# Large experts: gates and their turn between the two ways up, last combination by token halves, splits of the next stage issued in the last two experts

## Chip, cores and metric

One core of one Trainium2 chip. The metric is the device time of one execution in microseconds; the median of three runs of the kernel before is 2007.82 us.

## The reference, cut to what matters

The program is a chain of three blocks: a layer with attention and a dense feed-forward network, a layer with attention and eight large experts, and a hybrid block with 32 small experts. Only the large experts and the layer norm behind them are touched. Each of 256 tokens goes to its best two of eight experts of width 2816:

```python
def moe_swiglu(x, w_router, b_router, w_in, w_out):
    logits = (x2 @ w_router).astype(jnp.float32) + b_router.astype(jnp.float32)
    top_vals, top_idx = lax.top_k(logits, TOP_K)
    gates = jax.nn.softmax(top_vals, axis=-1)
    ...
    def expert_block(args):
        xb, e = args
        h = xb @ w_in[e]
        return (jax.nn.silu(h[:, :D_FF]) * h[:, D_FF:]) @ w_out[e]
    ...
    y = jnp.zeros_like(x2).at[slot_tok].add((ys * slot_gate[:, None]).astype(x2.dtype))

x = layer_norm(DN_ALPHA * x + ffn, ln_ffn_g[i], ln_ffn_b[i])
```

## The kernel before

The order of every engine's instructions is the order in which the program emits them; nothing is reordered later. Each engine, and each DMA queue, takes its own in that order. Nearly all DMAs are issued by SyncE (SP).

**Weights.** Two streams share SP. `Long` (L159) brings the weights of the large experts as tiles of 128 x 2816 floats, `wl`, 1408 KB each, through eight buffers; `get` hands out the next tile and `load` issues the next load as soon as the tile before the one in use is given up, so SP then waits for TensorE. `Stream` (L32) brings all other weights as tiles of 512 KB, `wr`, through four raw buffers at this point. Most of them are split into two parts, `ws`, the high one by a copy on ScalarE (L123) and the low one by a subtraction on VectorE (L124), through three split buffers here. `ahead` (L133) alternates loads and splits until a buffer is lacking; a raw buffer is used again once its tile has been split. A row of a layer norm keeps its raw buffer until the norm is finished. With `eager` set, each `get` calls `ahead` first.

**The stage `moe1`** (L1223). The end of the norm before, routing (logits, ranks, slots: one-hot `OH` of 256 tokens by 96 slots for each expert, gates `G`), and a gather: x is split into `xth` (ScalarE) and `xtl` (GpSimd, POOL), and 64 matmuls pick the tokens of all experts into `gx`. Then the loop over eight experts (L1372), with a ring of eight PSUM banks. An expert uses 24 tiles `wl`: eight for the first way up (`pa`, then Silu on ScalarE), eight for the second (`pb`, then the gating product on VectorE, L1383, and a block transpose on VectorE into `ehT`, L1384, for three groups `g` of 32 slots), and eight for the way down. Every matmul there is a 32-column one; four run beside each other on four column groups (`c`). Between the ways up and the way down stand `combine` of the expert before (its outputs `ey` by its turned gates `mOT`, added to x by VectorE, L1369) and `back` (L1330): VectorE multiplies the one-hot by the gate into `mog` (L1336), TensorE turns it in six transposes, and ScalarE copies it to `mOT`. The way down goes through 22 steps `j`, each over the three groups and four chunks (L1393 to L1402).

**The end of the stage** (L1407). Combine of the last expert, four adds of 512 columns over both token halves; `get` of the norm's rows, which calls `ahead`, since `eager` was set in the last expert: first blocks of the hybrid stage are loaded and split here, ahead of the norm's statistics in the queue of VectorE. The statistics come one by one (L517, L522), the norm of token half 0 at once (L530), that of half 1 in the next stage (`finish`). The hybrid stage (L2289) turns x (L321: transposes, `xh` on ScalarE, `xl` on VectorE) and multiplies.

Of the kernel before, what the change touches and what calls it, by code (L numbers as in the profile page):

```python
# [10 lines left out]
F32 = mybir.dt.float32  # L11
# [8 lines left out]
T = 256  # L20
D = 1024
# [1201 lines left out]
def moe1(k, A, x, alpha, before, br):  # L1223
# [3 lines left out]
    with ExitStack() as mo:  # L1227
# [8 lines left out]
        with ExitStack() as ro:  # L1236
            ro.enter_context(k.banks(g=2, t=2, acc=4))
            rp = ro.enter_context(k.pool(name="m1r", bufs=1))
            xth = rp.tile([128, 2, D], F32R, name="xth")
            xtl = rp.tile([128, 2, D], F32R, name="xtl")  # L1240
            xT = rp.tile([128, KD, T], F32, name="mxT")
            lg = rp.tile([128, 2, NE], F32, name="mlg")
            lgT = rp.tile([NE, T], F32, name="mlgT")

            def gather(q):

                for j in range(KD):
                    p = k.g() if j % 2 else k.t()
                    n = 4 * CAP
                    for i, src in enumerate((xth, xtl)):  # L1250
                        for tb in range(2):
                            w = src[:, tb].rearrange("p (c j) -> p j c", j=KD)[:, j]
                            k.pe.matmul(p[:, :n], w, OH[:, tb, 4 * q:4 * q + 4].rearrange("p e s -> p (e s)"),
                                        start=i == 0 and tb == 0, stop=i == 1 and tb == 1)
                    k.copy(gx[:, j, 4 * q:4 * q + 4], p[:, :n].rearrange("p (e s) -> p e s", e=4))

            (wr, _, _), = k.st.get("rt")
            k.long.load()
            for tb in range(2):
                turn_half(k, x, xT, tb)  # L1260
                if tb == 0:
                    before.finish()
                    ln = LayerNorm(k, x, 1.0, "nm")
                p = k.g()
                ts = slice(tb * 128, tb * 128 + 128)
                for j in range(8):
                    k.pe.matmul(p[:NE, :128], wr[:, j], xT[:, j, ts], start=j == 0, stop=j == 7)
                nc.vector.tensor_copy(lgT[:, ts], p[:NE, :128])
                k.pe.transpose(p[:, 256:256 + NE], lgT[:, ts], k.ident[:NE, :NE])
                nc.vector.tensor_add(lg[:, tb], p[:, 256:256 + NE], br)  # L1270
                nc.scalar.copy(xth[:, tb], x[:, tb])
                nc.gpsimd.tensor_sub(xtl[:, tb], x[:, tb], xth[:, tb].bitcast(F32))
            rank = ranks(k, rp, lg, NE, "m1")
            M = rp.tile([128, 2, NE], BF, name="mM")
            nc.vector.tensor_scalar(M, rank, 1.5, None, op0=OP.is_lt)
            pos, count = places(k, rp, M, NE)

            slot = rp.tile([128, 2, NE], F32, name="mslot")
            nc.vector.tensor_scalar(slot, M, -65536.0, 65536.0, op0=OP.mult, op1=OP.add)
            nc.vector.tensor_add(slot, slot, pos)  # L1280

            def places_of(a, b):
                n = b - a
                nc.vector.tensor_tensor(
                    OH[:, :, a:b], k.iota[:, :CAP].rearrange("p (u o s) -> p u o s", u=1, o=1).to_broadcast([128, 2, n, CAP]),
                    slot[:, :, a:b].rearrange("p b (e o) -> p b e o", o=1).to_broadcast([128, 2, n, CAP]), op=OP.is_equal)

            places_of(0, 4)
            nc.vector.tensor_scalar(over, pos, float(CAP) - 0.5, None, op0=OP.is_gt)
            cf = rp.tile([128, 1], F32, name="mcf")  # L1290
            nc.vector.tensor_reduce(out=cf, in_=count, op=OP.max, axis=AX.X)
            nc.vector.tensor_copy(cnt, cf)
            gather(0)
            places_of(4, NE)

            oh = rp.tile([128, 2, 2, NE], F32, name="moh")
            mx = rp.tile([128, 2, 8], F32, name="mmx")
            gs = rp.tile([128, 4, 2], F32, name="mgs")
            for i in range(2):
                nc.gpsimd.tensor_scalar(oh[:, i], rank, float(i), None, op0=OP.is_equal)  # L1300
            for tb in range(2):
                nc.vector.max(out=mx[:, tb], in_=lg[:, tb])
            nc.gpsimd.tensor_sub(gs[:, 0], mx[:, :, 1], mx[:, :, 0])
            nc.scalar.activation(gs[:, 1], gs[:, 0], AF.Exp)
            nc.gpsimd.tensor_scalar(gs[:, 0], gs[:, 1], 1.0, None, op0=OP.add)
            nc.vector.reciprocal(gs[:, 2], gs[:, 0])
            nc.gpsimd.tensor_mul(gs[:, 3], gs[:, 1], gs[:, 2])
            w2 = [gs[:, 2 + i].rearrange("p (b o) -> p b o", o=1).to_broadcast([128, 2, NE]) for i in range(2)]
            nc.gpsimd.tensor_mul(G, oh[:, 0], w2[0])
            nc.gpsimd.tensor_mul(oh[:, 1], oh[:, 1], w2[1])  # L1310
            nc.gpsimd.tensor_add(G, G, oh[:, 1])
            nc.gpsimd.tensor_mul(over, over, G)
            gather(1)
            for tb in range(2):
                nc.scalar.mul(x[:, tb], x[:, tb], alpha)
            nv = nc.values_load(cnt[0:1, 0:1], min_val=0, max_val=T)
            with tc.If(nv > CAP):  # L1317
                wi, wo = (A[n].rearrange("l e a b -> (l e) a b") for n in ("w_exp_in", "w_exp_out"))
                leftover(k, x, xT, over, NE, KF,
                         lambda e, j: [wi[ds(e, 1), :, i * DFF + j * 128:i * DFF + j * 128 + 128].rearrange(  # L1320
                             "o (k p) n -> (o p) k n", p=128) for i in range(2)],
                         lambda e, j: wo[ds(e, 1), j * 128:j * 128 + 128].rearrange("o p n -> (o p) n"))
# [4 lines left out]
        tl = lambda shape, name, bufs=1: ep.tile(shape, F32, name=name, tag=name, bufs=bufs)  # L1327
        H2 = HF // 2

        def back(e):  # L1330

            t = tl([128, NG, T], "mOT", 2)
            og = tl([128, 2, NG, 4, 32], "mog")
            for tb in range(2):
                src = OH[:, tb, e].bitcast(F32).rearrange("p (g o s) -> p g o s", g=NG, o=1)
                nc.vector.tensor_scalar(og[:, tb], src.to_broadcast([128, NG, 4, 32]), G[:, tb, e:e + 1], None, op0=OP.mult)  # L1336
            for a in range(0, NG, 2):
                p = bank()
                n = min(2, NG - a)
# [16 lines left out]
                                        start=j == 0, stop=j == KD - 1)  # L1356
            return ps

        def combine(y, OT, after=None):
            ps = [bank() for _ in range(4)]  # L1360
            for tb in range(2):
                for g in range(NG):
                    for c in range(4):
                        cs = slice(32 * c, 32 * c + 32)
                        k.pe.matmul(ps[c][:, tb * 256:tb * 256 + 256], OT[cs, g, tb * 128:tb * 128 + 128], y[cs, g],
                                    start=g == 0, stop=g == NG - 1)
            for c in range(4):
                r = x[:, :, c * 256:c * 256 + 256]
                nc.vector.tensor_add(r, r, ps[c].rearrange("p (b n) -> p b n", b=2))  # L1369

        last = None
        for e in range(NE):  # L1372
            h = tl([128, NG, HF], "eh")
            hT = tl([128, NG, KF, 32], "ehT")
            pa = up(e)
            for g in range(NG):
                for s in range(2):
                    nc.scalar.activation(h[:, g, s * H2:s * H2 + H2], pa[g][s], AF.Silu)  # L1378
            pb = up(e)
            for g in range(NG):  # L1380
                for s in range(2):
# [2 lines left out]
                nc.vector.transpose(hT[:, g], h[:, g].rearrange("p (r j) -> p j r", j=KF))  # L1384
            if last:
                combine(*last)
            OT = back(e)
            if e == NE - 1:
                k.st.eager = True
            y = tl([128, NG, 256], "ey", 2)  # L1390
            ps = [bank()[:, :256] for _ in range(NG)]
            w = None
            for j in range(KF):  # L1393
                ws = []
                for c in range(4):
                    i = (4 * j + c) % 11
                    if i == 0:
                        w = k.long.get(c == 0)
                    ws.append(w[:, i * 256:i * 256 + 256])
                for g in range(NG):  # L1400
                    for c in range(4):
                        k.pe.matmul(ps[g][32 * c:32 * c + 32], hT[:, g, j], ws[c], start=j == 0, stop=j == KF - 1)  # L1402
                k.long.load()
            for g in range(NG):
                nc.scalar.copy(y[:, g], ps[g])  # L1405
            last = y, OT
        combine(*last)  # L1407
        ln.take([w[0] for w in k.st.get(*ln.keys)])
        for n in range(2):
            for tb in range(2):  # L1410
                ln.add(tb, n, None)
    return ln


# [1385 lines left out]
```

## Time and profile before

| | |
|---|---|
| median of 3 runs | 2007.82 us (2001.58 to 2016.43) |
| the profiled execution | 2008.52 us |
| its span, first to last instruction | 2006.7 us |
| mean granted TensorE clock | 0.946 |
| TensorE busy (matmul) | 1781.4 us, 89% |
| VectorE, ScalarE, GpSimd busy | 702.7, 448.3, 372.6 us |
| moved by DMA | 515.99 MB, mean 257 GB/s |

Times in the rows are microseconds from the start of the span. PE is TensorE's matmul, PEld its weight load, DVE VectorE, ACT ScalarE, POOL GpSimd, SPq the issuing of DMAs by SyncE. A busy PE is one with matmuls in flight; the granted clock is given as a share of 2.4 GHz. Since a matmul in float32 is two instructions, 264 matmuls are 528 instructions.

### The profile page before, as it was taken

To read this page: it belongs to the slowest core of one execution; us is meant where nothing else is said; L and a number is where in the kernel's file an instruction comes from. 1 tells how busy PE (TensorE), PEld (TensorE's weight loads), DVE (VectorE), ACT (ScalarE), POOL (GpSimd) and SP (SyncE) were. 2 spreads that over 40 slices of the span, in tenths; PEclk is the share of its full clock that TensorE was granted. 3 is DMA by queue.
4 is the path that set the end of the run, shared out by engine and by line. 5 is a ranking of instruction groups with operands and counts; after the bars stand their busy time and mean duration, and the time that the engine had idled before them with its cause. 6 is when DMAs were issued, how large, how long until landed. Compare 5 with 4: busy or idle time off the path is not lost. (4 is left out here: it accounts for less than half of the span.)

```text
span 2006.7 us, 41916 instructions
## 1 busy us (share of the span) xinstructions
PE 1781.4 (89%) x18587; PEld 1186.4 (59%) x18587; DVE 702.7 (35%) x1079; ACT 448.3 (22%) x783; POOL 372.6 (19%) x636
## 2 busy tenths in 40 slices
PE   8989999898889898989898989879765989989886
PEld 7867887896644444444444444468544767776543
DVE  5558556554110202020202020256535575621102
ACT  5534443552100000000000000033323432211100
POOL 5312987101000000000000000063213242000001
PEclk9999999899999999999999999989877999979999
DMA  6526666447489797979797979375224233799997
GB/s 217 157 65 210 203 202 204 128 119 270 171 341 403 304 412 311 411 304 412 308 413 302 414 308 415 119 237 174 86 68 149 89 98 98 276 354 408 409 408 307
DMA packets 138588, 515.99 MB, mean 257 GB/s; under 512 B 22248, under 2 KB 51350, under 8 KB 112800
## 3 DMA queue, kind: packets, MB, share of 16 engines
q1 hardware_dynamic: 135120, 497.39, 66.4%
q0 software_dynamic: 3280, 15.83, 2.3%
q8 instruction: 149, 2.44, 0.5%
q14 instruction: 39, 0.32, 0.0%
HBM read 503.48 MB, written 7.87 MB: 255 GB/s over the span
## 5 line engine op out<-in xcount | busy, mean ns | idle before, releaser
L218 PE MATMUL bank_r<-wl,gx 128*32 128x352 f32 x6144 | 455.8, 459 | 1.4 <-PEq L1317 1.4
L218 PE MATMUL bank_g<-ws,xh 128*128 128x256 f32 (+2 forms) x1440 | 387.0, 349 | 11.8 <-DVE ws L124 4.1
L218 PEld LDWEIGHTS bank_r<-wl,gx 128*32 128x32 f32 x6144 | 190.9, 110 | 263.6 <-issue 229.4
L124 DVE TENSOR_TENSOR ws<-wr,ws 128x1024 fp32r<-128x1024 f32 (+1 forms) x200 | 257.2, 1297 | 144.6 <-ACT ws L123 144.3
L218 PEld LDWEIGHTS bank_g<-ws,xh 128*128 128x128 f32 x1440 | 256.1, 194 | 50.1 <-issue 6.9
L1383 DVE TENSOR_TENSOR eh<-eh,bank_r 128x352 f32<-128x352 f32 x48 | 22.9, 505 | 654.6 <-PE bank_r L218 654.0
L123 ACT ACTIVATE ws<-wr 128x1024 fp32r<-128x1024 f32 (+1 forms) x200 | 209.2, 1057 | 175.8 <-PE bank_g L218 111.6
L218 PE MATMUL bank_r<-wl,ehT 128*32 128x256 f32 x4224 | 241.8, 393 | 0.0
L218 PE MATMUL bank_g<-ws,xl 128*128 128x256 f32 (+2 forms) x720 | 234.8, 342 | 3.4 <-DVE xl L341 3.3
L218 PEld LDWEIGHTS bank_r<-wl,ehT 128*32 128x32 f32 x4224 | 130.2, 114 | 110.4 <-issue 13.1
L533 POOL TENSOR_SCALAR lnmv<-lnmv 128x1 f32<-128x1 f32 x10 | 7.7, 772 | 887.9 <-DVE lnmv L532 887.9
L218 PEld LDWEIGHTS bank_g<-ws,xl 128*128 128x128 f32 x720 | 139.8, 194 | 17.7 <-DVE xl L341 4.4
L218 PE MATMUL bank_g<-wr,xgx 128*32 128x256 f32 x864 | 65.3, 396 | 18.9 <-DMA wr<-in_expert_w_up_dram 7.1
L1344 ACT COPY mOT<-bank_r 128x512 f32<-128x512 f32 (+1 forms) x16 | 6.9, 482 | 299.5 <-PE bank_r L222 299.5
L1378 ACT ACTIVATE eh<-bank_r 128x352 f32<-128x352 f32 x48 | 22.3, 464 | 203.9 <-PE bank_r L218 198.8
L218 PE MATMUL bank_t<-xOH,x 128*128 128x128 f32 x256 | 63.3, 409 | 0.9 <-DVE xOH L2573 0.9
L218 PEld LDWEIGHTS bank_t<-xOH,x 128*128 128x128 f32 x256 | 61.8, 336 | 3.8 <-issue 2.9
L218 PEld LDWEIGHTS bank_g<-wr,xgx 128*32 128x32 f32 x864 | 30.4, 113 | 53.2 <-DMA wr<-in_expert_w_up_dram 12.4
L1405 ACT COPY ey<-bank_r 128x256 f32<-128x256 f32 x24 | 8.9, 372 | 231.9 <-PE bank_r L218 231.3
L218 PE MATMUL bank_g<-ws,hh 128*128 128x512 f32 x176 | 57.5, 399 | 0.0
L615 POOL TENSOR_TENSOR aP<-aP,ast 128x512 f32<-128x512 f32 (+1 forms) x20 | 24.9, 1243 | 173.3 <-DVE ast L613 132.1
L222 PE MATMUL bank_r<-ident,mog 128*128 128x128 f32 x48 | 14.1, 433 | 45.7 <-DVE mog L1336 45.7
(697 smaller groups left out, 2186.1 us busy)
## 6 DMA issues: line engine op xcount, KB each, us to landing
wl<-in_w_exp_in_dram SPq DMA_DIRECT2D x128, 1408.0 KB, 9.0
wl<-in_w_exp_out_dram SPq DMA_DIRECT2D x64, 1408.0 KB, 8.5
wr<-in_expert_w_gate_dram SPq DMA_DIRECT2D x56, 512.0 KB, 10.2
wr<-in_w_in_dram SPq DMA_DIRECT2D x54, 512.0 KB, 5.0
wr<-in_expert_w_down_dram SPq DMA_DIRECT2D x54, 512.0 KB, 10.2
wr<-in_expert_w_up_dram SPq DMA_DIRECT2D x52, 512.0 KB, 10.2
wr<-in_w_ffn_in_dram SPq DMA_DIRECT2D x44, 512.0 KB, 3.9
wr<-in_w_out_dram SPq DMA_DIRECT2D x24, 512.0 KB, 4.3
```

The source lines that it names most:

```text
L123: nc.scalar.activation(hv, v, AF.Copy)
L124: nc.vector.tensor_sub(lv, v, hv.bitcast(F32))
L218: self.nc.tensor.matmul(out, lhsT, rhs, start=start, stop=stop)
L222: self.nc.tensor.transpose(out, src, ident)
L533: nc.gpsimd.tensor_scalar(mv[:, 2:3], mv[:, 1:2], 1e-5, None, op0=OP.add)
L615: e.tensor_mul(P[:, hs, :nk], P[:, hs, :nk], st[:, 3, hs].rearrange("p (h o) -> p h o", o=1).to_broadcast([128, 2, nk]))
L1344: nc.scalar.copy(t[:, a:a + n], p[:, :n * 256].rearrange("p (g t) -> p g t", g=n))
L1378: nc.scalar.activation(h[:, g, s * H2:s * H2 + H2], pa[g][s], AF.Silu)
L1383: nc.vector.tensor_mul(v, v, pb[g][s])
L1405: nc.scalar.copy(y[:, g], ps[g])
```

## The change

What it does:

1. `gates(e)`: `mog` is written by VectorE before the first way up of its expert. `back`, the six transposes and the copies to `mOT`, stands between the two ways up; before, both stood after the combine.
2. In experts 6 and 7 `ahead` is called between the two ways up. `eager` is set only when the stage is over.
3. The way down takes its first four steps `j` as one piece, group by group; from the fifth on step by step as before.
4. The last combine works by token halves: for each half the matmuls, four adds of 256 columns, the statistics, and for half 0 the norm. The norm's rows are fetched ahead of it.
5. `xth` and `xtl` are stored in the order in which the gather reads them; the stride that was in its weight reads is now in the reads of x by ScalarE and GpSimd.
6. The logits are copied from PSUM by ScalarE instead of VectorE.

```diff
-            xth = rp.tile([128, 2, D], F32R, name="xth")
-            xtl = rp.tile([128, 2, D], F32R, name="xtl")
+            xth = rp.tile([128, 2, KD, 128], F32R, name="xth")
+            xtl = rp.tile([128, 2, KD, 128], F32R, name="xtl")
...
-                            w = src[:, tb].rearrange("p (c j) -> p j c", j=KD)[:, j]
-                            k.pe.matmul(p[:, :n], w, OH[:, tb, 4 * q:4 * q + 4].rearrange("p e s -> p (e s)"),
+                            k.pe.matmul(p[:, :n], src[:, tb, j], OH[:, tb, 4 * q:4 * q + 4].rearrange("p e s -> p (e s)"),
...
-                nc.vector.tensor_copy(lgT[:, ts], p[:NE, :128])
+                nc.scalar.copy(lgT[:, ts], p[:NE, :128])
...
-                nc.scalar.copy(xth[:, tb], x[:, tb])
-                nc.gpsimd.tensor_sub(xtl[:, tb], x[:, tb], xth[:, tb].bitcast(F32))
+                xv = x[:, tb].rearrange("p (c j) -> p j c", j=KD)
+                nc.scalar.copy(xth[:, tb], xv)
+                nc.gpsimd.tensor_sub(xtl[:, tb], xv, xth[:, tb].bitcast(F32))
...
-        def back(e):
-
-            t = tl([128, NG, T], "mOT", 2)
+        def gates(e):
+
             og = tl([128, 2, NG, 4, 32], "mog")
...
+            return og
+
+        def back(og):
+
+            t = tl([128, NG, T], "mOT", 2)
...
-        def combine(y, OT, after=None):
+        def combine(y, OT, norm=None):
...
+                if norm:
+                    for c in range(4):
+                        r = x[:, tb, c * 256:c * 256 + 256]
+                        nc.vector.tensor_add(r, r, ps[c][:, tb * 256:tb * 256 + 256])
+                        if c % 2:
+                            norm.add(tb, c // 2, None)
+            if norm:
+                return
...
+            og = gates(e)
             pa = up(e)
...
+            OT = back(og)
+            if e >= NE - 2:
+                k.st.ahead()
             pb = up(e)
...
-            OT = back(e)
-            if e == NE - 1:
-                k.st.eager = True
...
-            for j in range(KF):
-                ws = []
-                for c in range(4):
-                    i = (4 * j + c) % 11
-                    if i == 0:
-                        w = k.long.get(c == 0)
-                    ws.append(w[:, i * 256:i * 256 + 256])
+
+            for js in [range(0, 4)] + [range(j, j + 1) for j in range(4, KF)]:
+                ws = {}
+                for j in js:
+                    for c in range(4):
+                        i = (4 * j + c) % 11
+                        if i == 0:
+                            w = k.long.get(len(ws) == 0)
+                        ws[j, c] = w[:, i * 256:i * 256 + 256]
                 for g in range(NG):
-                    for c in range(4):
-                        k.pe.matmul(ps[g][32 * c:32 * c + 32], hT[:, g, j], ws[c], start=j == 0, stop=j == KF - 1)
+                    for j in js:
+                        for c in range(4):
+                            k.pe.matmul(ps[g][32 * c:32 * c + 32], hT[:, g, j], ws[j, c], start=j == 0, stop=j == KF - 1)
                 k.long.load()
...
-        combine(*last)
         ln.take([w[0] for w in k.st.get(*ln.keys)])
-        for n in range(2):
-            for tb in range(2):
-                ln.add(tb, n, None)
+        combine(*last, norm=ln)
+    k.st.eager = True
     return ln
```

## Rows read from the trace of the kernel before

**Rows 1.** Timeline of TensorE: start, length, instructions, [idle time before, its end].

```profile
524.03 57.01 PE L218 MATMUL bank_r<-wl,gx 128*32 128x352 f32 x768 [1.41 <-PEq L1317]
...
674.90 2.87 PE L218 MATMUL bank_r<-ey,mOT 32*128 32x256 f32 x48
683.44 1.76 PE L222 MATMUL bank_r<-ident,mog 128*128 128x128 f32 x6 [5.67 <-DVE mog L1336]
...
1299.23 2.87 PE L218 MATMUL bank_r<-ey,mOT 32*128 32x256 f32 x48
```

**Rows 2.** Timeline of VectorE at the turn of expert 1.

```profile
673.31 1.79 DVE L1384 STREAM_TRANSPOSE ehT<-eh 128x704 f32<-128x704 f32 x1
...
675.97 1.79 DVE L1384 STREAM_TRANSPOSE ehT<-eh 128x704 f32<-128x704 f32 x1
...
678.63 1.79 DVE L1384 STREAM_TRANSPOSE ehT<-eh 128x704 f32<-128x704 f32 x1
...
682.70 1.12 DVE L1336 TENSOR_SCALAR mog<-mOH,mG 128x384 f32<-128x384 f32 x2
```

**Rows 3.** Windows: stretch, length, five engines' busy time, granted clock, DMA share, GB/s.

```profile
715.65:772.50 56.85, 56.85 (x772) 22.92 (x764) 2.58 (x3) 3.35 (x8) 0.00 (x0) 1.00 1.01 415
685.10:689.00 3.90, 3.90 (x41) 1.80 (x44) 0.00 (x0) 0.57 (x2) 0.00 (x0) 0.50 0.00 0
```

**Rows 4.** Timeline of TensorE's weight loads in the way down of expert 1.

```profile
688.97 26.36 PEld L218 LDWEIGHTS bank_r<-wl,ehT 128*32 128x32 f32 x488 [0.23 <-issue]
```

**Rows 5.** Timeline of ScalarE at the end of a first way up.

```profile
643.69 3.42 ACT L1378 ACTIVATE eh<-bank_r 128x352 f32<-128x352 f32 x6 [25.07 <-PE bank_r L218]
```

**Rows 6.** The page's DMA issues: count, KB each, median us to landing.

```profile
wl<-in_w_exp_in_dram SPq DMA_DIRECT2D x128, 1408.0 KB, 9.0
...
wr<-in_w_in_dram SPq DMA_DIRECT2D x54, 512.0 KB, 5.0
```

**Rows 7.** Timeline after the last combine, all engines.

```profile
1302.12 2.48 DVE L1369 TENSOR_TENSOR x<-x,bank_r 128x512 f32<-128x512 f32 x4 [35.02 <-PE bank_r L218]
...
1305.77 6.52 SPq L107 DMA_DIRECT2D wr<-in_w_in_dram  x3
1309.58 1.06 ACT L123 ACTIVATE ws<-wr 128x1024 fp32r<-128x1024 f32 x1 [7.93 <-DMA wr<-in_w_in_dram]
1310.67 1.23 DVE L124 TENSOR_TENSOR ws<-wr,ws 128x1024 fp32r<-128x1024 f32 x1 [3.79 <-ACT ws L123]
1311.81 1.87 DVE L522 BATCH_NORM_STATS2 lnst<-x 128x6 f32<-128x512 f32 x3
...
1313.71 0.21 DVE L532 BATCH_NORM_AGGREGATE lnmv<-lnst 128x2 f32<-128x12 f32 x1
...
1316.37 1.09 PE L222 MATMUL bank_t<-ident,x 128*128 128x128 f32 x4 [14.27 <-DVE x L539]
...
1318.19 0.67 DVE L341 TENSOR_TENSOR xl<-bank_t,xh 128x512 fp32r<-128x512 f32 x1
```

**Rows 8.** Timeline of routing and gather, all engines.

```profile
490.95 2.33 POOL L1272 TENSOR_TENSOR xtl<-x,xth 128x1024 fp32r<-128x1024 f32 x1
491.01 2.82 DVE L539 SCALAR_TENSOR_TENSOR x<-x,lnmv,wr 128x512 f32<-128x512 f32 x1 [0.75 <-POOL lnmv L534]
...
498.21 1.05 ACT L1271 CAST xth<-x 128x1024 fp32r<-128x1024 f32 x1
...
515.72 0.64 PE L218 MATMUL bank_g<-mOH,xth 128*128 128x384 f32 x2
...
521.51 0.64 PE L218 MATMUL bank_g<-mOH,xth 128*128 128x384 f32 x2
```

**Rows 9.** Groups by line, shapes kept apart: count, busy us, mean ns, idle before.

```profile
L218 PEld LDWEIGHTS bank_g<-mOH,xtl 128*128 128x128 f32 x16 | 4.7, 339 | 0.0
...
L218 PEld LDWEIGHTS bank_g<-ws,oh 128*128 128x128 f32 x32 | 6.0, 188 | 1.5 <-issue 0.2
...
L340 ACT CAST hy<-bank_t 128x512 fp32r<-128x512 f32 x2 | 2.0, 1097 | 3.5 <-PE bank_t L222 3.5
```

More of the change, by code (lines that the diff above doesn't have):

```diff
@@ L1386, in moe1 @@
                 combine(*last)
-            OT = back(e)
-            if e == NE - 1:
-                k.st.eager = True
             y = tl([128, NG, 256], "ey", 2)
             ps = [bank()[:, :256] for _ in range(NG)]
-            w = None
-            for j in range(KF):
-                ws = []
-                for c in range(4):
-                    i = (4 * j + c) % 11
-                    if i == 0:
-                        w = k.long.get(c == 0)
-                    ws.append(w[:, i * 256:i * 256 + 256])
+            for js in [range(0, 4)] + [range(j, j + 1) for j in range(4, KF)]:
[6 more added lines that the diff above has]
+                        ws[j, c] = w[:, i * 256:i * 256 + 256]
                 for g in range(NG):
-                    for c in range(4):
-                        k.pe.matmul(ps[g][32 * c:32 * c + 32], hT[:, g, j], ws[c], start=j == 0, stop=j == KF - 1)
+                    for j in js:
+                        for c in range(4):
+                            k.pe.matmul(ps[g][32 * c:32 * c + 32], hT[:, g, j], ws[j, c], start=j == 0, stop=j == KF - 1)
                 k.long.load()
```

## The prediction

> **What bounds the kernel now.** I read TensorE's timeline through the eight experts first, then VectorE's at one turn, then clock and supply by stretches, and last the two ends of the stage. The eight experts take from 524.03 to 1299.23, 775.2 us of the profiled execution, 96.9 us each [rows 1]. TensorE never waits for a weight tile there: the two ways up are one unbroken run of 57.0 us, and the way down follows at its own pace. The only hole is the turn between them: after the combine (2.87 us) TensorE stands still for 5.67 us, until the gated one-hot `mog` is written, turns it in 1.76 us and only then begins the way down [rows 1]. VectorE shows why: its queue holds multiply and transpose of three slot groups, then the adds of the combine, then `mog`, which is done at 683.8, 8.8 us after the last way-up matmul, though nothing that it reads is new. The first third of `ehT`, all that the way down needs to begin, is there at 675.1 [rows 2].
>
> The hole costs a second time: in the stretch after it the granted clock is 0.50, the lower level (1.2 GHz), and TensorE had been idle before the fall [rows 3]. At the full level 488 instructions of the way down take 26.36 us, 0.0540 us each [rows 4]; all 528 would take 28.5 us.
>
> The weight supply is close behind: in the ways up the DMA engines are busy throughout, at 415 GB/s [rows 3]. A tile is 1408 KB (1.442 MB), so at that rate one comes every 3.47 us, and TensorE uses one every 57.0/16 = 3.56 us. A whole expert averages 24 x 1.442 MB / 96.9 us = 357 GB/s.
>
> **The change, part by part.**
>
> *Gates and turn.* `mog` is now written on VectorE before the first way up, which gives it over 50 us. The six transposes stand between the two ways up. I take half the 1.76 us for them, 0.9 us: that row is at the lower clock, and TensorE is now busy before them. Could the second way up then wait for banks? It takes those of the first one, so it needs the six Silu. They run from 643.69 to 647.1 in an expert whose first way up ends at 674.9 - 28.5 = 646.4 [rows 5], in the order in which the banks are wanted, and the transposes cover 0.9 us. Nothing is added: a gain is not possible, the upper bound is 0.7 us for each expert.
>
> *Way down by groups.* It begins right after the combine: four steps of group 0, then of 1, then of 2. A group is 4 steps x 4 chunks x 2 instructions x 0.054 = 1.73 us. From a combine's end at 677.8 group 1 is wanted at 679.5 and group 2 at 681.2; `ehT` has them at 677.8 and 680.4 [rows 2]. No wait. Without a combine (expert 0) VectorE's chain leaves about 2.0 us: group 2 is ready 5.5 us after the ways up and 1.7 us follow, against 5.2 us of work.
>
> *Sum of the loop.* An expert: 56.9 + 0.9 + 2.9 + 28.5 = 89.2 us; expert 0: 56.9 + 0.9 + 28.5 + 2.0 = 88.3. Together 7 x 89.2 + 88.3 = 712.7, a gain of 775.2 - 712.7 = 62.5 us. The supply that this needs is 24 x 1.442 MB / 89.2 us = 388 GB/s, under the 415 shown.
>
> *Splits ahead.* The call in expert 6 can load the norm's second row and the first hybrid block (two buffers are free since the norm), then blocks 1, 2 and 3, each through the buffer of the block before it and after its split. That fills the three split buffers, so the call in expert 7 issues nothing. What counts is SP: it issues in order, and the expert's weights stand behind these loads. With P the end of expert 6's first way up, SP reaches them when tile 6 is done, P - 3.6, and issues block 0 by P - 2.8, behind two to three tiles in flight, whose landing takes 9.0 us [rows 6]; with 2.5 us for the two short loads it lands at P + 8.5. A split is 1.06 + 1.2 us, ACT then VectorE [rows 7], both without other work then, 2.4 us with the hand-over; a short load lands after 5.0 us [rows 6]. Three splits and two landings: 8.5 + 7.2 + 10.0 = P + 25.7. Then block 3 and tile 15 are issued: 2.0 MB at 415 GB/s are 4.7 us, and some 2.5 us of latency (3.8 us, 1305.77 to 1309.58, less 1.3 for 0.5 MB) [rows 7], so P + 33. TensorE holds tiles 8 to 14 and wants tile 15 at P + 0.9 + 7 x 3.56 = P + 25.8: a stall of some 7 us. Low bound: landings of 3.8 us and a light queue in front, 0. High bound: a full 9 us landing at the end, 11 us, and 2 us of lower clock, 13. I take 7.5, nearest to the medians. After it tiles come every 3.47 us and are used every 3.56, with the combine as extra, so no second stall. ACT's and VectorE's next work (down copies, gating) comes later than the last split.
>
> *Last combination by halves.* With S the start of the last combine (1299.23), the first norm's aggregate ran at 1313.71, S + 14.5, behind adds, splits and a block's landing [rows 7]. Now: first half of the combine 1.4, four half adds of some 0.4 (0.62 at full width), two statistics of 0.65, so S + 4.4; the transposes 2.7 us later, S + 7.1, where they were at S + 17.1. But VectorE then has norm 0 (3.9 us) and the second half's adds and statistics (2.9 us) ahead of the split of the turned x: `xl`, at 1318.19 before (S + 19.0), starts at S + 11.2 [rows 7]. Gain 7.8; from 5 (other waits of the hybrid stage take over) to 10 (the transposes' shift). The hybrid stage's own loads stand behind the same waits, so it moves as a block.
>
> *Start of the stage.* The gather's 64 matmuls read weights at a stride: 24 of them, from 515.72 to 521.51, are 0.241 us apart [rows 8], with weight loads of 339 ns against 188 ns for packed ones [rows 9]. 384 columns need 0.16 us at the full clock (2.4 GHz), so I take 0.17: some 52 matmuls outside the lower clock x 0.07 = 3.6 us; below, 0, if the load was never the limit. Against it: the stride is now in the reads of ACT and POOL (a strided ACT cast of 512 took 1097 ns [rows 9], where 1024 packed took 1.05 us [rows 8], so `xth` takes 1.05 to 2.1), and the second `xth` waits on ACT behind the logit copy, near 500.5 instead of 498.21, so that POOL's `xtl` runs into VectorE's ranking. When `xtl` ran at 490.95 for 2.33 us, VectorE's normalise, started at 491.01, took 2.82 us and ended 0.5 us after POOL's end [rows 8]. So 2 to 3 us go back. Net gain 1.0, from +4 to -3.
>
> The Trainium skill, "SBUF — State Buffer", section "Who interferes with whom", says that a VectorE instruction with two SBUF inputs and a GpSimd one that reads SBUF shut each other out for a whole instruction. By that rule, with which the 2.82 us row agrees, the part is worth 1 us, without it some 3.5.
>
> For a strided subtract on POOL no row has a price. The Trainium skill, "GPSIMD Engine Reference", section "7. Performance pitfalls for Q7 kernels", gives 50% more for reads at steps over 8 bytes, an estimate of 3.5 us, which would take the gain of 1.0 to about 0.
>
> **Sum.** 62.5 - 7.5 + 7.8 + 1.0 = 63.8 us off the profiled execution's 2008.5 us: 1944.7. The median of the runs shown, 2007.8, is 0.7 lower: I say 1944. Its own range: best 62.5 + 2 - 0 + 10 + 4 = 78.5 (1930; the 2 if the combine's tail overlaps), worst 60.5 - 13 + 5 - 3 = 49.5 (1959).
>
> **Rivals.**
> - *The hold costs nothing* (0.15): the seven tiles suffice. 1937. For it: a short load takes little alone; against: the first stands behind full tiles.
> - *The hold lasts through expert 7* (0.12): its backlog of seven tiles meets engines that deliver one per 4.0 us; 24 x 0.45 = 11 us more: 1955. Against: 415 GB/s over 57 us.
> - *The end gives nothing* (0.08): the hybrid stage is held by its own loads; 1952.
> - *The supply sets the period* (0.05), the other side: if the engines can't pass their present average of 357 GB/s, each expert keeps 97 us and the loop gains nothing, and SP's 28 us without expert loads (P - 2.8 to P + 25.7) are lost less the 2.6 MB moved in them (7 us): 2008 + 21 - 9 = 2020, slower. It decides below 388 GB/s; 415 speaks against it.
> - *The hole only moves* (0.04): the way down waits for `ehT`; half of the loop's gain, 1975. Against: 680.4 against 681.2.
>
> **How the numbers follow.** The forecast has 0.56. Its range 1930 to 1959 holds the first three rivals; with some 5 us for the spread of the runs shown (2001.6 to 2016.4), 1925 to 1964, which leaves out the last two and tails, under 2 in 10. A measurement here tells about 1%, 20 us, from no change. Faster by over 1% (under 1988): all but the fourth, less a margin, 0.92. Within 1%: 0.05, the fourth above all. Slower: 0.03, the fourth with a longer hold.
>
> **What would show it.** TensorE's timeline: six transposes of under 1 us between two runs of some 28.5 us, combine followed by the way down without idle time, 528 instructions in 28.5 us at clock 1.00, 89 us from expert to expert. In expert 6 one wait of TensorE for a `wl` tile late in the second way up, SP's loads of it behind hybrid blocks. First x transposes 7 us after the last combine's start. Gather matmuls 0.17 us apart. Wrong would be: waits for `wl` in every expert, idle time ahead of groups 1 and 2, or a second way up that waits for Silu.

## The result and the profile after

The changed kernel takes 1946.54 us in the median of four runs (1945.17 to 1947.03), the kernel before took 2007.95 us beside it (2001.58 to 2016.43). The ratio is 0.9691 with a 95% interval of 0.9654 to 0.9727: faster by 3.1%. The forecast was 1944 us, its range 1925 to 1964.

| | before | after |
|---|---|---|
| span of the profiled execution | 2006.7 us | 1944.7 us |
| TensorE busy (matmul) | 1781.4 us, 89% | 1763.3 us, 91% |
| mean granted TensorE clock | 0.946 | 0.958 |
| the eight experts, to the last combine | 775.2 us | 722.7 us |
| an expert (mean of 1 to 5) | 97.3 us | 89.17 us |

The prediction's 96.9 us is the mean of all eight experts; expert 0, which has no combine in front, took 94.0 us before the change.

TensorE's timeline after, at the turn of expert 1, answers to [rows 1] (start, length, instructions, then in brackets the idle time before and what ended it):

```profile
613.53 28.61 PE L218 MATMUL bank_r<-wl,gx 128*32 128x352 f32 x384
642.08 0.87 PE L222 MATMUL bank_r<-ident,mog 128*128 128x128 f32 x6
642.88 28.61 PE L218 MATMUL bank_r<-wl,gx 128*32 128x352 f32 x384
671.42 2.87 PE L218 MATMUL bank_r<-ey,mOT 32*128 32x256 f32 x48
674.22 28.70 PE L218 MATMUL bank_r<-wl,ehT 128*32 128x256 f32 x528
702.73 28.58 PE L218 MATMUL bank_r<-wl,gx 128*32 128x352 f32 x384
731.25 0.87 PE L222 MATMUL bank_r<-ident,mog 128*128 128x128 f32 x6
```

No bracket stands in these lines: TensorE never waits here. The six transposes take 0.87 us between the ways up, where they took 1.76 us behind a hole of 5.67 us [rows 1]. The way down follows the combine at once and takes 28.70 us. VectorE's last `ehT` answers to [rows 2]:

```profile
675.13 1.79 DVE L1400 STREAM_TRANSPOSE ehT<-eh 128x704 f32<-128x704 f32 x1
676.85 2.44 DVE L1381 TENSOR_TENSOR x<-x,bank_r 128x512 f32<-128x512 f32 x4
679.20 1.13 DVE L1335 TENSOR_SCALAR mog<-mOH,mG 128x384 f32<-128x384 f32 x2
```

The third group is ready at 676.92. At the 1.73 us a group that the prediction counted, TensorE comes to it at 677.68: 0.76 us to spare. `mog`, now that of the next expert, still stands at the end of VectorE's queue, but nobody wants it before its turn at 731.25, 51 us later.

Windows of the same expert, for [rows 3] (stretch, length, five engines' busy time, granted clock, DMA share, GB/s):

```profile
674.30:702.70 28.40, 28.40 (x528) 17.11 (x532) 6.00 (x9) 0.52 (x2) 0.00 (x0) 1.00 0.90 354
702.70:760.00 57.30, 57.30 (x775) 25.35 (x770) 2.06 (x3) 4.24 (x10) 0.00 (x0) 1.00 1.00 407
```

The clock is at its upper level throughout the way down, and in the ways up the DMA engines are busy all the time at 407 GB/s. The weights keep up, but with little in reserve.

Expert 6 is the exception. TensorE's timeline:

```profile
1088.74 25.06 PE L218 MATMUL bank_r<-wl,gx 128*32 128x352 f32 x336
1118.97 6.44 PE L218 MATMUL bank_r<-wl,gx 128*32 128x352 f32 x48 [5.17 <-DMA wl<-in_w_exp_in_dram]
```

SP's, the issuing of DMAs, in the same stretch:

```profile
1085.41 25.19 SPq L107 DMA_DIRECT2D wr<-in_w_in_dram  x4
1110.70 0.46 SPq L186 DMA_DIRECT2D wl<-in_w_exp_in_dram  x1
```

ScalarE's, the first halves of the splits:

```profile
1095.60 1.06 ACT L123 ACTIVATE ws<-wr 128x1024 fp32r<-128x1024 f32 x1 [6.05 <-DMA wr<-in_w_in_dram]
1101.66 1.06 ACT L123 ACTIVATE ws<-wr 128x1024 fp32r<-128x1024 f32 x1 [5.00 <-DMA wr<-in_w_in_dram]
1107.90 1.06 ACT L123 ACTIVATE ws<-wr 128x1024 fp32r<-128x1024 f32 x1 [5.18 <-DMA wr<-in_w_in_dram]
```

SP stands behind four hybrid blocks for 25 us, because three of them need the buffer of a block that has first to land and be split. Only then does it issue the load of tile 15. 336 instructions are seven tiles of 48: TensorE runs dry before tile 15, waits 5.17 us, and after that takes 6.44 us for a tile that elsewhere takes 3.58. A window there shows why, the lower level of the clock after the wait:

```profile
1119.00:1122.00 3.00, 3.00 (x24) 1.05 (x28) 0.90 (x2) 0.00 (x0) 0.00 (x0) 0.50 1.01 424
```

The last combine and the first transposes of x, for [rows 7]:

```profile
1245.95 1.58 PE L218 MATMUL bank_r<-ey,mOT 32*128 32x256 f32 x24
1248.02 1.03 PE L218 MATMUL bank_r<-ey,mOT 32*128 32x256 f32 x4 [0.49 <-DVE x L1374]
1249.40 2.30 PE L218 MATMUL bank_r<-ey,mOT 32*128 32x256 f32 x20 [0.35 <-DVE x L1374]
1253.10 1.09 PE L222 MATMUL bank_t<-ident,x 128*128 128x128 f32 x4 [1.39 <-DVE x L539]
```

With S the start of the last combine, the transposes come at S + 7.15, where they came at S + 17.1 [rows 7].

### The profile page after: what moved, and what is told of

It is laid out like the page before. It is cut to its first block, busy times and chain, and to the rows that moved or that the text cites. A ratio compares the mean times of both kernels' runs of the same rounds, so it can differ in the third digit from the quotient of the medians.

```text
span 1944.7 us, 41930 instructions
## 1 busy us (share of the span) xinstructions
PE 1763.3 (91%) x18587; PEld 1200.5 (62%) x18587; DVE 709.1 (36%) x1081; ACT 450.3 (23%) x785; POOL 375.5 (19%) x636
## 3 DMA queue, kind: packets, MB, share of 16 engines
q8 instruction: 149, 2.44, 0.5%
## 5 line engine op out<-in xcount | busy, mean ns | idle before, releaser
L218 PE MATMUL bank_r<-wl,gx 128*32 128x352 f32 x6144 | 462.2, 462 | 7.6 <-DMA wl<-in_w_exp_in_dram 5.2
L218 PEld LDWEIGHTS bank_r<-wl,gx 128*32 128x32 f32 x6144 | 205.4, 111 | 257.9 <-issue 220.5
L218 PE MATMUL bank_r<-wl,ehT 128*32 128x256 f32 x4224 | 230.0, 379 | 1.7 <-DVE ehT L1400 1.5
L218 PEld LDWEIGHTS bank_r<-wl,ehT 128*32 128x32 f32 x4224 | 139.8, 110 | 91.0 <-issue 5.5
L218 PE MATMUL bank_g<-ws,oh 128*128 128x512 f32 x128 | 44.6, 411 | 0.0
L1400 DVE STREAM_TRANSPOSE ehT<-eh 128x704 f32<-128x704 f32 x24 | 43.0, 1791 | 0.8
```

What stands on the lines that cost most here:

```text
L218: self.nc.tensor.matmul(out, lhsT, rhs, start=start, stop=stop)
```

## The experiments

Each ran beside the kernel before on the same chip; ratios are to that. Experiments 1 to 4, 5 to 8 and 9 to 11 ran on three chips, so kernels are compared across these sets by their ratios, or by distances inside one trace. What lies ahead of this stage moves by up to 7 us between traces whose edits all come later; the start of the stage is therefore given from the last norm's aggregate on VectorE (L532; from 484.70 to 492.09, 489.34 in the changed kernel). The stretch behind the last combine moves too: in the nine traces that end as the changed kernel does it lasts 698.8 to 701.8 us.

**1. The multiplication and the turn back behind the combine**, the rest of the change kept:

```diff
-            og = gates(e)
             pa = up(e)
...
-            OT = back(og)
...
             if last:
                 combine(*last)
+            OT = back(gates(e))
```

> The changed kernel with the gates and the turn put back behind the combine; all else as changed. Theory (VectorE's queue makes TensorE wait for mog, and the idle time lowers the clock): each of experts 1 to 7 gets back 5.7 us of idle time, 0.9 us of slower transposes and 1 to 2 us of a slower way down, expert 0 some 5 us; about 57 us more than the changed kernel, near 2003 us, with some 97 us from expert to expert. Rival (the gain came from the way down by groups and from weights asked for earlier): under 1975 us.

2008.49 us, ratio 0.9995 (0.9983 to 1.0007): nothing of the gain is left. The hole is back with its old size:

```profile
677.72 2.87 PE L218 MATMUL bank_r<-ey,mOT 32*128 32x256 f32 x48
686.26 1.76 PE L222 MATMUL bank_r<-ident,mog 128*128 128x128 f32 x6 [5.67 <-DVE mog L1335]
687.95 31.01 PE L218 MATMUL bank_r<-wl,ehT 128*32 128x256 f32 x528
```

In expert 6 the wait for a weight tile is still there (5.59 us), so the loop takes 785.0 us, 9.8 more than before, and the end gives back 7.4. The loss against the changed kernel, some 61 us, is a little over the 57 expected. All the other parts of the change together come to nothing without the first.

**2. Only the turn back behind the combine**, `mog` still early:

```diff
-            OT = back(og)
...
             if last:
                 combine(*last)
+            OT = back(og)
```

> The changed kernel with mog still written ahead of the first way up, but the six transposes put back behind the combine. Theory (only the moment at which VectorE writes mog matters): no idle time at the turn, 89.2 us from expert to expert, 1946 us within 3. Rival (the place of the transposes on TensorE matters too, by a lower clock or by the wait of the way down for banks): 1 to 2 us more for each expert, 1955 to 1961 us.

1947.52 us, ratio 0.9694 (0.9673 to 0.9714), as the changed kernel's. An expert takes 89.03 us; the transposes take the same 0.87 us behind the combine. The place of the turn is indifferent. What counts is when `mog` is written.

**3. The way down step by step from its start:**

```diff
-            for js in [range(0, 4)] + [range(j, j + 1) for j in range(4, KF)]:
+            for js in [range(j, j + 1) for j in range(KF)]:
```

> The changed kernel with the way down step by step from its first step, as before the change. Theory (the groups hide VectorE's multiply and transpose of groups 1 and 2): TensorE waits some 1.8 us for ehT of group 2 in experts 1 to 7 (ready 5.5 us after the ways up, wanted 0.9 us after the combine's end at 2.8) and 2.6 us more in expert 0: 15 us more, near 1961 us. Rival (the combine covers the chain, the groups bring nothing): 1946 us, at most 1950.

1966.73 us, ratio 0.9788 (0.9768 to 0.9809). TensorE's way down of expert 1:

```profile
680.14 1.07 PE L218 MATMUL bank_r<-wl,ehT 128*32 128x256 f32 x16
682.99 27.83 PE L218 MATMUL bank_r<-wl,ehT 128*32 128x256 f32 x512 [1.78 <-DVE ehT L1400]
```

Two groups of the first step, then 1.78 us of waiting for the third of `ehT`, as expected. The price is higher than expected (20 us against some 15): an expert takes 91.16 us, 2.0 more, and expert 0, which has no combine to cover it, 94.78 in place of 90.25. Of these 4.5 us, 2.2 are longer waits for `ehT`, near the 2.6 expected; most of the rest is the lower clock, which the expectation left out: it was 0.52 from 590 to 594, behind the waits, and the last 512 instructions took 29.74 us against 27.83 in the later experts. Expert 6, where the hold stands in the way, isn't longer. That makes 16.2 us in the loop. The first way up starts 1.4 us later in this trace, but so does the aggregate ahead of it (490.89, 1.55 later), so that is not the edit's. The rest of the kernel is 3 us longer, 701.8 us, which lies within what other traces with the same end show (experiment 4 has 701.7), so nothing ties it to the edit.

**4. Fewer blocks ahead in expert 6:**

```diff
             if e >= NE - 2:
-                k.st.ahead()
+                k.st.ahead(4 if e < NE - 1 else 1 << 30)
```

> The changed kernel with two of the three splits issued in expert 6 and the third, with the load of the block after it, in expert 7. Theory (SP's queue: the expert's weights wait behind loads that wait for splits, longer than seven tiles last): SP is held until some 10 us after the first way up of expert 6 and for about as long in expert 7, both under the 25 us that seven tiles last; no wait for a wl tile, about 8 us less than the changed kernel, 1938.5 us. Rival (the splits cost TensorE time by their own work or by their bytes, wherever they stand): 1944 to 1947 us.

1939.86 us, ratio 0.9646 (0.9621 to 0.9671), and no wait for a tile in any expert; expert 6 takes 89.17 us like the others. The expectation had the split wrong: all three splits stay in expert 6, only the load of the block behind them moves to expert 7. SP shows it:

```profile
1085.11 19.57 SPq L107 DMA_DIRECT2D wr<-in_w_in_dram  x3
1104.77 0.46 SPq L186 DMA_DIRECT2D wl<-in_w_exp_in_dram  x1
...
1173.80 0.39 SPq L107 DMA_DIRECT2D wr<-in_w_in_dram  x1
```

Tile 15 is issued at 1104.77 in place of 1110.70. From the end of the first way up (0.3 us earlier here) that is 5.6 us sooner, more than the wait of 5.17 us, so the wait goes, with the lower clock behind it. One load fewer ahead in a shared queue was worth the whole hold of 8 us: the loop takes 714.6 us against 722.7.

**5. Six buffers for the weights of the large experts in place of eight** (`LONG1 = 4` in place of 6, the two others being added elsewhere).

> Everything of the change, with six buffers for weight tiles in place of eight. Theory (the hold of expert 6 is SP standing behind hybrid blocks while TensorE uses up the tiles in hand; elsewhere the supply is ahead): two tiles fewer in hand, so the wait for a wl tile in expert 6 comes two tiles earlier and grows by 2 x 3.56 = 7.1 us, from 5.2 to some 12.3, and no other expert waits: 1946.5 + 7.1 = 1953.7 us. Rival (the supply is near its limit at 89 us an expert and lives on its buffers): waits for wl in every expert, over 1960 us.

1953.12 us, ratio 0.9719 (0.9703 to 0.9735). In expert 6 TensorE runs dry two tiles earlier, after five in place of seven:

```profile
1087.95 17.96 PE L218 MATMUL bank_r<-wl,gx 128*32 128x352 f32 x240
1116.92 12.73 PE L218 MATMUL bank_r<-wl,gx 128*32 128x352 f32 x144 [11.02 <-DMA wl<-in_w_exp_in_dram]
```

The other experts don't wait and keep their 89.17 us. So the supply is not near its limit at this pace; what empties the buffers is SP standing still. The wait grew by 5.9 us, a little less than the 7.1 expected.

**6. Nothing ahead in the last experts; splits from the last way down on, as before:**

```diff
-            if e >= NE - 2:
-                k.st.ahead()
...
+            if e == NE - 1:
+                k.st.eager = True
```

> The change without its third part: no hybrid block is loaded or split in the experts 6 and 7 ahead of time; as before, the splits are issued from the last way down on. Theory: the wait in expert 6 goes (8 us less), and the end loses what the splits ahead had brought, with the first x transposes near S + 15 in place of S + 7.1 (S the start of the last combine; 8 us more): 1946 us, within 2. So the third part pays nothing in this form. Rivals: the splits ahead are worth more than their hold (over 1950), or nothing (1938).

1948.38 us, ratio 0.9691 (0.9675 to 0.9708), the same as the changed kernel's. The two sides of the trade stand in one trace: the last combine starts at 1238.12, 7.8 us earlier, and its second half waits again behind the splits on VectorE:

```profile
1238.12 1.58 PE L218 MATMUL bank_r<-ey,mOT 32*128 32x256 f32 x24
1247.18 4.63 PE L218 MATMUL bank_r<-ey,mOT 32*128 32x256 f32 x24 [7.48 <-DVE x L1374]
1252.26 1.09 PE L222 MATMUL bank_t<-ident,x 128*128 128x128 f32 x4 [0.45 <-DVE x L539]
```

The transposes come at S + 14.1, the first `xl` (1256.25) at S + 18.1 in place of S + 11.1. As built, the third part of the change buys 7 us at the end for 8 us in expert 6; only with experiment 4 does it pay.

**7. The split of x for the gather ahead of the router's matmuls:**

```diff
+                xv = x[:, tb].rearrange("p (c j) -> p j c", j=KD)
+                nc.scalar.copy(xth[:, tb], xv)
+                nc.gpsimd.tensor_sub(xtl[:, tb], xv, xth[:, tb].bitcast(F32))
                 p = k.g()
                 ts = slice(tb * 128, tb * 128 + 128)
```

> The change with ACT's and POOL's split of x for the gather issued ahead of the router's matmuls, so that ACT doesn't hold the second half of xth behind the copy of the logits. Theory (POOL's xtl beside VectorE's ranking cost 2.6 us on the row of mslot): xtl of the second half runs before 502.5, mslot takes 0.2 in place of 2.78 us, the gather begins some 1.5 us earlier, near 505.3, and the time is 1945 us, too little for the interval; it is read in the profile. Rival (the row of mslot is long for another reason): it stays at 2.8 us, the gather stays at 506.8.

1946.10 us, ratio 0.9679 (0.9663 to 0.9695), within the interval of the changed kernel's. In the profile the gather begins 16.35 us after the aggregate, where the changed kernel needs 17.49: 1.1 us earlier, not 1.5, and the first way up 33.4 against 33.9. POOL's timeline of the changed kernel:

```profile
502.53 2.84 POOL L1272 TENSOR_TENSOR xtl<-x,xth 128x1024 fp32r<-128x1024 f32 x1 [7.33 <-ACT xth L1271]
```

Its VectorE:

```profile
502.62 2.78 DVE L1279 TENSOR_SCALAR mslot<-mM 128x16 f32<-128x16 bf16 x1
```

POOL with the split ahead:

```profile
502.49 2.84 POOL L1265 TENSOR_TENSOR xtl<-x,xth 128x1024 fp32r<-128x1024 f32 x1 [5.87 <-ACT xth L1264]
```

VectorE with the split ahead:

```profile
504.03 1.45 DVE L1215 TENSOR_TENSOR m1eq<-mlg 128x128 f32<-128x128 f32 x1
...
506.77 0.18 DVE L1279 TENSOR_SCALAR mslot<-mM 128x16 f32<-128x16 bf16 x1
```

Both times the VectorE instruction that begins while `xtl` runs ends with it: `mslot` at 505.40 (POOL 505.37), `m1eq` at 505.48 (POOL 505.33). Away from `xtl`, `mslot` takes 0.18 us. The wait is moved and shortened, not removed.

**8. The last combination whole, adds and statistics behind it, the splits still ahead:**

```diff
-        combine(*last, norm=ln)
+        combine(*last)
+        for n in range(2):
+            for tb in range(2):
+                ln.add(tb, n, None)
```

> The change with the last combination whole, as for the other experts, and the adds and the norm's statistics behind it; the splits stay ahead. Theory (most of the end's gain comes from the splits having left VectorE's and SP's queues, not from the halves): the first x transposes come near S + 9.9 in place of S + 7.1, xl near S + 11.9 in place of S + 11.1, so 1 to 2.8 us more: 1947.5 to 1949 us. Rival (the halves carry the gain): xl near S + 15 or later, over 1950 us.

1948.73 us, ratio 0.9698 (0.9678 to 0.9717). The first `xl` starts at 1257.21, S + 11.7 (S = 1245.54), against S + 11.1 with halves. So the halves are worth 0.5 us where it counts, though the first transposes come 2.7 us earlier with them (S + 7.15 against S + 9.85). The time can't tell the two kernels apart, as their intervals overlap.

**9. The kernel before with one edit: `mog` ahead of the first way up:**

```diff
             hT = tl([128, NG, KF, 32], "ehT")
+            og = gates(e)
...
-            OT = back(e)
+            OT = back(og)
```

> The kernel before with one edit: the multiplication that writes mog stands on VectorE ahead of the first way up; the turn of mog stays behind the combine, the way down goes step by step, and the start, the end and the splits are as before. Theory (the hole had two parts: 5.67 us of waiting for mog, with the lower clock after it, and 1.8 us for the last third of ehT behind it): the wait for mog goes, the turn takes 0.9 us and covers half of the 1.8 us, so an expert takes 90.0 to 91.1 us in place of 96.9 and the loop some 730 to 733 of 775.2: 42 to 45 us less, 1963 to 1966 us. Rivals: the hole only moves (half the gain, near 1985), or all of the loop's gain is in this one edit (1946).

1963.24 us, ratio 0.9761 (0.9742 to 0.9781). This one edit takes 47.2 us out of the loop (523.83 to 1251.85, 728.0 us). An expert takes 90.69 us; what remains is one wait:

```profile
676.66 0.87 PE L222 MATMUL bank_r<-ident,mog 128*128 128x128 f32 x6
677.46 1.07 PE L218 MATMUL bank_r<-wl,ehT 128*32 128x256 f32 x16
679.97 27.83 PE L218 MATMUL bank_r<-wl,ehT 128*32 128x256 f32 x512 [1.44 <-DVE x L1373]
```

It ends with an add of the combine (L1373), not with the last `ehT`, which is done 0.6 us earlier, at 677.55 + 1.79 = 679.34. The ring of eight banks fits this: with the turn behind the combine, the third bank of the way down is the eighth after the first of the combine, which the first add gives back (679.26 and a quarter of 2.44 us are 679.87). In experiment 3 the turn stands ahead, so this bank is one of the second way up, and there the wait ends with `ehT`. No run varies the number of banks.

**10. Experiments 4 and 7 together, with `xtl` taken by VectorE in place of POOL:**

```diff
+                nc.vector.tensor_sub(xtl[:, tb], xv, xth[:, tb].bitcast(F32))
```

> The change with fewer loads in expert 6 (as in e4_spread), and with the split of x for the gather issued ahead of the router's matmuls and its difference xtl taken by VectorE in place of POOL. Theory (POOL's xtl beside VectorE's work cost 2.5 us at the last normalise and 2.6 at mslot): the last normalise takes 0.75 us, mslot 0.2, xtl on VectorE fits into its idle time, the gather begins some 4 us earlier and so does the first way up, near 519.3 in place of 523.28; expert 6 has no wait: 1936 us, 4 below e4_spread. Rivals: VectorE's strided difference costs as much as it saves (1940), or the first way up is held by something else and stays near 523 (1940).

1934.69 us, ratio 0.9630 (0.9614 to 0.9646): the lowest median of all. VectorE's last normalise in the changed kernel, beside POOL's first `xtl`:

```profile
492.53 3.22 DVE L539 SCALAR_TENSOR_TENSOR x<-x,lnmv,wr 128x512 f32<-128x512 f32 x1
```

Of VectorE's start in experiment 10, these lines:

```profile
487.89 0.75 DVE L539 SCALAR_TENSOR_TENSOR x<-x,lnmv,wr 128x512 f32<-128x512 f32 x1
488.56 2.02 DVE L1265 TENSOR_TENSOR xtl<-x,xth 128x1024 fp32r<-128x1024 f32 x1
...
495.69 0.17 DVE L1279 TENSOR_SCALAR mslot<-mM 128x16 f32<-128x16 bf16 x1
```

The last normalise takes 0.75 us in place of 3.22 and `mslot` 0.17. The first way up begins 28.7 us after the aggregate, against 33.9: 5.2 us, a little over the 4 expected. The absolute 513.41 is no measure, as this trace's aggregate is at 484.70. The gain on experiment 4 is 0.0016 in the ratio, 3 us, and the two intervals overlap.

**11. The start of the stage undone**, x in its own order, strided weights, logits copied by VectorE.

```diff
-                            k.pe.matmul(p[:, :n], src[:, tb, j], OH
+                            w = src[:, tb].rearrange("p (c j) -> p j c", j=KD)[:, j]
+                            k.pe.matmul(p[:, :n], w, OH
...
-                nc.gpsimd.tensor_sub(xtl[:, tb], xv, xth[:, tb].bitcast(F32))
+                nc.gpsimd.tensor_sub(xtl[:, tb], x[:, tb], xth[:, tb].bitcast(F32))
```

> The change without its edits of the stage's start: xth and xtl in the order of x, the gather's weights read at a stride, the logits copied by VectorE. Theory (3 to 4 us gained in the gather, 2 to 3 lost again in front of it): gather matmuls 0.241 us apart in place of 0.1735, the gather begins near 505.3 in place of 506.8, mslot takes 0.2 us, the first way up begins 0.8 to 1.0 us later than in the changed kernel, and the time is 1947.5 us, within 2. Rivals: the edits of the start are worth the whole 3.6 us (1950) or cost time (1944).

1945.81 us, ratio 0.9682 (0.9661 to 0.9703): the time can't tell it from the changed kernel. In the trace the first way up starts 34.7 us after the aggregate against 33.9, so 0.8 us are lost as expected. That is one trace against another: the seven others with the changed start have 33.8 to 35.0, the three with the old one 34.5 to 34.8, so the 0.8 us is no larger than the spread. But something else is won, and that is clear. TensorE's first way up in the changed kernel:

```profile
523.28 30.30 PE L218 MATMUL bank_r<-wl,gx 128*32 128x352 f32 x384 [2.47 <-PEq L1317]
```

The same with the start undone:

```profile
524.74 28.61 PE L218 MATMUL bank_r<-wl,gx 128*32 128x352 f32 x384 [1.29 <-PEq L1317]
```

Windows of the changed kernel, just behind the pause:

```profile
523.30:525.30 2.00, 2.00 (x20) 0.94 (x24) 1.02 (x2) 1.28 (x1) 0.00 (x0) 0.60 0.04 8
525.30:527.30 2.00, 2.00 (x20) 0.96 (x16) 0.00 (x0) 0.00 (x0) 0.00 (x0) 0.55 0.00 0
```

With the start undone:

```profile
524.80:526.80 2.00, 2.00 (x28) 1.03 (x32) 1.00 (x2) 1.90 (x3) 0.00 (x0) 1.00 0.05 12
```

In the changed kernel the granted clock falls to 0.60 and 0.55 from 523.3 to 527.3, after a pause of 2.47 us; with the longer gather the pause is 1.29 us and the clock stays at 1.00. That costs 1.7 us. It is so in every trace: the ten with the packed gather have pauses of 2.08 to 2.50 us and lose the 1.7 us, the three with the strided one have pauses of 1.00 to 1.41 us and don't. Whether the longer pause or the denser gather ahead of it brings the fall, no run separates. Up to the second way up, the edits of the start come out 0.9 us behind in this pair of traces.

## Why the prediction was right, step by step

The sum was made against the profiled execution; the spans differ by 2006.7 - 1944.7 = 62.0 us.

| term | forecast | measured |
|---|---|---|
| loop without the hold | 62.5 | 775.2 - (722.7 - 8.1) = 60.6 |
| hold in expert 6 | -7.5 | 89.17 - 97.23 = -8.1 |
| from the last combine to the end | +7.8 | 707.5 - 698.8 = +8.7 |
| start of the way up | +1.0 | 524.03 - 523.28 = +0.8 |
| sum | 63.8 | 62.0 |

The measured terms are from one trace each. The end is good to about 2 us (698.8 to 701.8 us in the traces with the changed end, 707.5 and 709.7 in the two with the old one), and the start is no larger than its spread.

*Gates and turn, way down by groups.* Right in size: 89.2 us an expert forecast, 89.17 measured; transposes 0.9 and 0.87; no wait for banks, none for `ehT`. Experiments 1, 2, 3 and 9 show it part by part: `mog` early is 47 of the some 61 us alone, and without it the rest is worth nothing; the groups take away the last wait, 1.5 to 2 us an expert. Where the turn stands doesn't matter, which the prediction had not said. The 47 us are also more than the eight holes, 45.8 us, although new waits come. In experts 1 to 7 experiment 9 gains 6.6 us an expert: 5.7 of hole, 0.9 of the turn and, by difference, some 1.5 of the way down, both now at a clock of 1.00, less the new wait of 1.4. In expert 0 it gains only 0.9 us: two waits for `ehT` (1.54 and 2.02 us) take the hole's place, and the clock falls behind them (0.50 from 588 to 592).

*Expert 0.* Mis-sized by 2.0 us: forecast 88.3, measured 90.25 (613.53 - 523.28). The 2.0 us allowed for `ehT` came in the main (0.22, 0.77 and 0.72 us of waits), but its first way up ran at the lower clock for 4 us, which experiment 11 ties to the edits of the start. The prediction took the full level there because [rows 1] showed it, and missed that with the shorter gather the pause ahead of the way up is longer.

*The hold.* Right mechanism, place and tile, 7.5 against 8.1, with two errors that nearly cancel. With P = 1088.0, the end of expert 6's first way up, TensorE wanted tile 15 at P + 25.8, as forecast; it was there at P + 31.0, not P + 33. SP issued it at P + 22.7, not P + 25.7, mainly because the splits followed each other by 6.1 to 6.2 us, not 7.4 (landings of w_in had 4.1 us in the median after, 5.0 before [rows 6]); from there TensorE had it after 8.3 us, not 7.2. But 2.9 us of lower clock followed the wait, which the prediction had in its high bound alone. Experiments 4 and 5 show the cause: issue tile 15 5.6 us earlier and the hold is gone; take two tiles away and the wait doubles.

*The end.* 7.8 forecast; `xl` came 7.9 us earlier after S, and the tail is 8.7 us shorter in all. Experiments 6 and 8 divide it: some 7 us come from the loads and splits that no longer stand in the last combine's way (experiment 6 puts both back, on SP, ScalarE and VectorE), 0.5 from the halves. The prediction's sum held both without saying which carries it, and put the halves first.

*The start.* Close as a start of the way up (1.0 against 0.8), but partly by luck. The gather is as forecast: matmuls 0.173 us apart, 13.98 us in place of 17.35, so 3.4 us gained of 3.6. It begins 1.5 us later after the aggregate (17.49 against 16.01), where 2 to 3 were forecast; against experiment 11 it is 2.0. The rest of what is given back, 1.1 us, is the longer pause behind the gather (2.47 against 1.41 us), a term that the prediction doesn't have; what sets its length stays open. Nor did it follow the part into expert 0, where the 1.7 us are lost; up to there it was a small loss, not a gain. The row of 1097 ns, by which the prediction bounded a strided read of ACT, has its stride in what it writes (`hy`); its bound of 2.1 us held all the same, at 2.04. The lock that the prediction put into "the ranking" sat on `mslot`, 2.78 us. The Trainium skill, "SBUF — State Buffer", section "Who interferes with whom", counts `tensor_scalar` among the instructions that can take the port pair shared with GpSimd, where its operands meet the conditions of a two-port mode, although it has one input. The rows agree: `mslot` takes 0.18 and 0.17 us away from `xtl` (experiments 7 and 10) and 2.78 beside it.

*The rivals.* That the supply sets the period fell: no expert but 6 waits for a tile, even with six buffers. So did the hold through expert 7: one wait, in expert 6, and expert 7 takes 89.3 us (1156.66 to 1245.95). That the hold costs nothing fell with the 8.1 us in expert 6. That the end gives nothing, and that the hole only moves, fell by the table and by the timeline.

## What to carry to other kernels

Look first for an instruction whose inputs are long there but which stands late in an in-order queue: emitting it before the long stretch brought three quarters of this gain in a single edit. Before loads or splits are put ahead of time into a queue that also feeds the bound engine, count how long the queue will stand still and compare it with what is buffered: here one load fewer turned a trade of 7 for 8 us into 7 us of gain. A part that shortens a stage also changes the pauses next to it, so it is priced to the end of the next stretch of TensorE, not to its start: here a way up that began some 0.8 us earlier ended 0.9 us later.

## What the runs showed beyond that

- A pause of TensorE cost more than itself in three places, each with the granted clock at the lower level behind it: 5.17 us, then 2.9 more in expert 6 (1.6 to 3.0 in the eight traces that have this wait); 5.67 us, then a way down of 31.0 in place of 28.7 us (experiment 1); 2.47 us, then 1.7 more in expert 0. Single pauses of 1.44 us (experiment 9) and 1.78 us (experiment 3) at the start of a way down cost only themselves: it kept a clock of 1.00.
- A VectorE instruction on 16 numbers a partition can take 2.78 us: it ends when POOL's instruction beside it ends.
- A strided read costs each engine something else. For 128 x 1024 float32 with steps of 32 bytes: ScalarE 2.04 us against 1.05 [rows 8]; POOL's subtraction with one such input 2.84 against 2.33 [rows 8], 22% more (the Trainium skill, "GPSIMD Engine Reference", section "7. Performance pitfalls for Q7 kernels", gives some 50% for a read at such steps, which this row doesn't reach); VectorE's 2.02 (experiment 10), where the splits of weights, without a stride, take 1.22. TensorE pays for a strided weight load instead: matmuls 0.241 us apart against 0.173.
